# 168 products that nothing reads, put behind the last gated product of an encoder trunk

## The chip, the cores and the metric

The kernel runs on one core of one Trainium2 chip (trn2). The metric is the device time of one execution in microseconds (us); less is better. A core has five engines that work through a queue of instructions each: TensorE (PE; its weight loads are shown apart as PEld), VectorE (DVE), ScalarE (ACT), GpSimd (POOL) and SyncE (SP), which issues most DMAs here.

## The reference, cut to what matters

Two layers of attention, gates and a feed-forward network over 256 tokens of width 2048, all in float32. The change stands at the very end, behind the last gated embedding product and beside the last norm:

```python
for i in range(DEPTH):
    ...
    e = p[i] @ w_ple_in[i]
    x = x + jax.nn.sigmoid(rmsnorm(x, g_ple[i]) @ w_ple_gate[i]) * e
return rmsnorm(x, g_final)
```

`rmsnorm(x, g)` is `x * rsqrt(mean(x*x) + eps) * g`. The output is 1 x 256 x 2048.

## The kernel before

Activations are kept transposed: `xT` holds x as 16 chunks of 128 partitions (features) by 256 tokens. A product of 128 output features therefore runs over 16 chunks of the contraction, and its result, 128 x 256, gathers in one PSUM bank.

To get float32 accuracy out of a faster matmul type, every operand is held as two parts, a rounded high part and the rest. For activations the two stand side by side in one tile of 512 columns: `ua[j]` and `ub[j]` (16 tiles each), high part in columns 0 to 255, low part in 256 to 511. For weights `piece` (L159) loads 128 x 1024 floats into `w`, ScalarE makes `whi`, and VectorE makes `wlo`. `emit` (L191) then issues, for each chunk, the kernel's own form: one matmul with `whi` as the stationary operand over all 512 columns (L199), which gives high x high in the first half of the bank and high x low in the second; and one with `wlo` over the 256 high columns (L200), which adds low x high to the second half. A branch of it (L195 to L197, `whole`) does the same with three matmuls of 256 columns into one half. The two halves are added later by `joined` (ScalarE copies one half, VectorE adds the other).

Products go through four PSUM banks in turn (`ps_mm`). The value products (L385 to L387) have activations as the stationary operand and 512 columns of weights as the moving one. Attention scores (L334) take both operands from activation tiles (`fa`, `fb`, `ub`, `kr`).

The stage around the change is the last loop of the second layer: 16 gated products (L676 to L687), each with a sigmoid on ScalarE, a multiply with `es` and an add to `xT` on VectorE, and then `add(n)` (L670), which squares the chunk into one of two sums and scales the chunk by `g_final`. The last of the 16 uses the `whole` form. After the loop, `norm` (L259) sums the squares over partitions with four fp32 matmuls of one column (L264), VectorE works out the reciprocal root, `spread` (L267) brings it to all partitions with one fp32 matmul of 128 x 256 (L273), and six multiplies over `xT` (L72, called from L690 to L693) are each followed by an output DMA from SyncE.

The order of each engine's queue is set by the Tile framework's scheduler, which orders instructions by a timeline of its own; dependencies between engines become semaphore waits. `tt` (L71) is the helper behind most VectorE operations, so many of these carry the line L72.

Of the kernel before, what the change touches and what calls it, by code (L numbers as in the profile page):

```python
# [13 lines left out]
F32R = mybir.dt.float32r  # L14
I32 = mybir.dt.int32
AF = mybir.ActivationFunctionType
# [3 lines left out]
P = 128  # L20
T = 256
# [15 lines left out]
PT = 8  # L37
# [13 lines left out]
def encoder(ctx, tc, x, p, positions, cols, lams, wq, wk, wv, wcq, wckv, wkr, wga, wgb,  # L51
            w_q_up, w_kn, w_v, w_bd, w_bm, w_out, w_gate, w_up, w_down, w_pin, w_pg, rope_c, out):
    nc = tc.nc
    V, A, PE = nc.vector, nc.scalar, nc.tensor
# [3 lines left out]
    wts = pool("wts")  # L58
    tmp = pool("tmp")
    stat = pool("stat")  # L60
    ps_mm = pool("ps_mm", 4, space=PSUM)
# [6 lines left out]
    def bank(ps=ps_at, tag="at", name="at", shape=(P, 2 * T)):  # L68
        return ps.tile(list(shape), F32, tag=tag, name=name)

    def tt(o, a, b, op):  # L71
        return V.tensor_tensor(out=o, in0=a, in1=b, op=op)  # L72
# [4 lines left out]
    def ts(o, a, s1, s2, op0, op1=ALU.bypass):  # L77
        return V.tensor_scalar(out=o, in0=a, scalar1=s1, scalar2=s2, op0=op0, op1=op1)


    ua = [const.tile([P, 2 * T], F32R, name=f"ua{j}") for j in range(NC)]
    ub = [const.tile([P, 2 * T], F32R, name=f"ub{j}") for j in range(NC)]
# [11 lines left out]
    xT = const.tile([P, NC, T], F32, name="xT")  # L94
# [4 lines left out]
    at = 0  # L99
# [19 lines left out]
    def tables():  # L119
        V.tensor_copy(posf, posi)  # L120
        got = []
        for i, name in enumerate("pm"):
            ang, k, r, a = (aside[j + i][:, m, :] for j in (1, 3) for m in range(2))
            ts(ang, posf, rc[:, 2 * i : 2 * i + 1], None, ALU.mult)
            ts(k, ang, 1.0 / TWO_PI, ROUND, ALU.mult, ALU.add)
            ts(k, k, ROUND, None, ALU.subtract)
            stt(r, k, -C1, ang, ALU.mult, ALU.add)
            stt(r, k, -C2, r, ALU.mult, ALU.add)
            stt(r, k, -C3, r, ALU.mult, ALU.add)
            ts(r, r, PI_IN, -PI_IN, ALU.min, ALU.max)  # L130
            stt(a, r, -1.0, r, ALU.mult, ALU.min)
            ts(a, a, math.pi / 2, None, ALU.add)
            cs = const.tile([P, T], F32, name="cos_" + name)
            sn = const.tile([P, T], F32, name="sin_" + name)
            A.activation(cs, a, AF.Sin)
            A.activation(sn, r, AF.Sin)
            ts(sn, sn, rc[:, 2 * i + 1 : 2 * i + 2], None, ALU.mult)
            got += [cs, sn]
        return got
# [62 lines left out]
    def product(src, us, whole=False):  # L202


        acc = bank(ps_mm, "mm", "mm")
        n = len(us)
        for a in range(0, n, PT):
            m = min(PT, n - a)
            hi, lo = piece(src[:, a * P : (a + m) * P], m)
            emit(acc, hi, lo, 0, us[a : a + m], a == 0, a + m == n, whole)  # L210
        return acc[:, :T] if whole else acc
# [15 lines left out]
    def joined(acc, o=None):  # L227
        t = scratch("join", 3)
        A.activation(t, acc[:, T:], AF.Copy)  # L229
        o = scratch("a", 4) if o is None else o  # L230
        tt(o, acc[:, :T], t, ALU.add)
        return o
# [7 lines left out]
    def rsqrt(src, n, eps, width):  # L240

        v, y, a = (stat.tile([P, 2 * DH], F32, tag="r" + s, name="r" + s, bufs=2)[:, :width] for s in "vya")
        ts(v, src, 1.0 / n, eps, ALU.mult, ALU.add)
        ts(y.bitcast(I32), v.bitcast(I32), -0.5, 1597463007.0, ALU.mult, ALU.add)
        for _ in range(3):
            stt(a, y, -0.5, y, ALU.mult, ALU.mult)
            tt(a, a, v, ALU.mult)
            stt(y, a, 1.5, y, ALU.add, ALU.mult)
        return y

    def square_into(acc, src, first):
        if first:
            A.activation(acc, src, AF.Square)
        else:
            sq = scratch("sq", 2)
            A.activation(sq, src, AF.Square)
            tt(acc, acc, sq, ALU.add)

    def norm(sums, n):  # L259

        s = bank()
        for j, a in enumerate(sums):
            for b in range(2):
                PE.matmul(s[:, b : b + 1], a[:, b * P : (b + 1) * P], ones[:, 0:1], start=j + b == 0, stop=j + b == len(sums))  # L264
        return rsqrt(s[:, 0:2], n, EPS, 2)

    def spread(col, copied=True):  # L267

        dg = stat.tile([P, 2, P], F32, tag="dg", name="dg", bufs=1)
        for b in range(2):  # L270
            ts(dg[:, b, :], ident, col[:, b : b + 1], None, ALU.mult)
        s = bank()
        PE.matmul(s[:, :T], ones, dg, start=True, stop=True)  # L273
        if not copied:
            return s[:, :T]
        row = stat.tile([P, T], F32, tag="row", name="row", bufs=2)
        A.activation(row, s[:, :T], AF.Copy)  # L277
        return row

    def normed(sums, one, two):  # L280

        got = [joined(one())]
        col = norm(sums, DM)
        got.append(joined(two()))
        return spread(col), col, got
# [4 lines left out]
    def stream(us, gain):  # L290

        acc = squares()

        def add(c):
            split(us[c], xT[:, c, :], g(gain, c))
            square_into(acc, xT[:, c, :], c == 0)

        return acc, add
# [70 lines left out]
    def values(src, us, load=None):  # L369
# [3 lines left out]
        for half in range(2):  # L373
# [18 lines left out]
            if not half:  # L392
                yield vals


    warm = bank()
    for _ in range(WARM):
# [7 lines left out]
    for L in range(DEPTH):  # L405

        steps = values(wv[L], ua, None if L else load)
        for vd in steps:
            if L == 0 and vd is not None:
# [3 lines left out]
                with after_splits():  # L413
                    rcol = norm([sq0[0][:, j, :] for j in range(2)], DM)
                    next(steps)
                    R = spread(rcol)
                    cos_p, sin_p, cos_m, sin_m = tables()
                    lambdas()
                break
            if L:  # L420
                next(steps)
                rcol = norm([acc], DM)
                next(steps)
                R = spread(rcol)
                break
# [5 lines left out]
        for o, t in ((cr, cos_p), (sr, sin_p), (crm, cos_m), (srm, sin_m)):  # L431
            tt(o, t, R, ALU.mult)

# [17 lines left out]
        def latent(us, w, raws):  # L451
            ss = squares()
            for c in range(len(us)):
                tt(raws[c], joined(product(w[L, c], ua)), R, ALU.mult)
                square_into(ss, raws[c], c == 0)
# [55 lines left out]
        def gate(w, store, n):  # L511
            tt(store(n), joined(product(w[L, n], ua)), R, ALU.mult)

# [115 lines left out]
        acc, add = stream(ub, f"g_ffn{L}")  # L629
# [4 lines left out]

        R, _, pre = normed([acc], lambda: product(w_gate[L, 0], ub), lambda: product(w_up[L, 0], ub))
        pT, es = ua[14:], []
# [4 lines left out]
        for part, (f0, f1) in enumerate(FF_PARTS):  # L641
# [11 lines left out]
            if last:  # L653
                acc, add = stream(ub, f"g_ple{L}")
# [10 lines left out]
        R, _, pre = normed([acc], lambda: product(w_pg[L, 0], ub), lambda: product(w_pg[L, 1], ub))  # L665
# [8 lines left out]
        else:  # L674
            acc, add = stream(ua, f"g_mix{L + 1}")
# [11 lines left out]
            add(n)  # L687

    R = spread(norm(sums, DM), copied=False)
    for n, m in ((0, 1), (1, 1), (2, 2), (4, 4), (8, 4), (12, 4)):  # L690
        o = xT[:, n : n + m, :]
        tt(o, o, R[:, None, :].to_broadcast([P, m, T]), ALU.mult)
        nc.sync.dma_start(out[:, n : n + m, :], o)  # L693
# [84 lines left out]
```

## Time and profile before

| | us |
|---|---|
| median of 2 runs | 2939.7 (2939.02 to 2940.39) |
| the profiled execution's own time | 2939.35 |
| its span, first to last instruction | 2937.4 |
| TensorE busy | 2918.8 |
| VectorE busy | 2039.8 |
| ScalarE busy | 1520.5 |

The profile is of one execution. A page of it gives the busy time of each engine, the chain of work that ended last, and groups of equal instructions. A group's line reads: line of the code, engine, operation, output <- inputs, shape, count | busy time, mean of one in ns | idle time before. Matmuls are pipelined and their ends are modelled, so the durations of neighbours overlap; the pace is read from starts, or from counts in a window. Rows of the timeline begin with the start and the duration in us; what stands in brackets is the idle time of the engine before the row and what ended it. Rows of the chain have a start, a length and what the chain went through. Rows of the windows have the stretch, its length, busy time and count for PE, PEld, DVE, ACT and POOL, then the granted TensorE clock, the DMA share and GB/s.

### The profile page before, as it was taken

What the parts mean: (1) busy time and instruction counts of PE and PEld (TensorE: products, weight loads), DVE (VectorE), ACT (ScalarE), POOL (GpSimd) and SP (SyncE); (2) the same over time, 40 slices, a digit from 0 to 9 for tenths busy, and PEclk for the clock granted to TensorE, in tenths of its full rate; (3) what the DMA queues carried; (4) which work ended last, traced back from release to release, by engine and by line L of the source; (5) the groups of instructions that cost most, each with busy time, mean ns of one, the idle gap of its engine ahead of it and who ended that gap; (6) DMA issues with size and microseconds to landing.
All of it is one profiled execution on the core that took longest, in us unless ns stands there. A gap on an engine that the chain in (4) does not pass through costs nothing.

```text
span 2937.4 us, 45159 instructions
## 1 busy us (share of the span) xinstructions
PE 2918.8 (99%) x17390; PEld 2583.1 (88%) x17390; DVE 2039.8 (69%) x3447; ACT 1520.5 (52%) x2512; POOL 3.5 (0%) x11
## 2 busy tenths in 40 slices
PE   9999999999999999999999999999999999999998
PEld 7998888888888888888889988888888888888887
DVE  7887658776666656666858875587666666566676
ACT  6576545554444444444646755455444444444454
POOL 0000000000000000000000000000000000000000
PEclk9999999999999999999999999999999999999999
DMA  6544455555565566566554444555556655655654
GB/s 229 166 159 144 158 188 192 188 185 187 182 194 187 177 191 195 188 188 187 187 186 160 152 151 165 187 192 188 185 188 183 193 187 180 193 187 188 188 186 141
DMA packets 155751, 532.47 MB, mean 181 GB/s; under 512 B 16928, under 2 KB 23584, under 8 KB 155536
## 3 DMA queue, kind: packets, MB, share of 16 engines
q1 hardware_dynamic: 154944, 528.55, 56.1%
q8 instruction: 136, 2.23, 0.3%
q0 software_dynamic: 160, 0.46, 0.1%
q10 hardware_dynamic: 432, 0.59, 0.1%
q14 instruction: 79, 0.65, 0.1%
HBM read 527.43 MB, written 2.10 MB: 180 GB/s over the span
## 4 chain that ended last, share of the span: by engine, by line
PE 99%; DVE 0%; DMA 0%; ACT 0%; SPq 0%; issue 0%; DVEq 0%
PE mm L199 56%; PE mm L200 29%; PE mm L195 3%; PE mm L197 3%; PE mm L196 3%; PE S L334 1%; PE mmv L385 1%; PE mmv L386 1%; PE mmv L387 1%; PE at L352 0%; PE at L552 0%; PE at L609 0%; DMA w<-in_wv 0%; PE at L273 0%; DVE xT L72 0%; PE at L312 0%
## 5 line engine op out<-in xcount | busy, mean ns | idle before, releaser
L72 DVE TENSOR_TENSOR wlo<-w,whi 128x1024 fp32r<-128x1024 f32 (+2 forms) x1029 | 1229.4, 1195 | 785.3 <-ACT whi L169 772.6
L169 ACT ACTIVATE whi<-w 128x1024 fp32r<-128x1024 f32 (+2 forms) x1029 | 1066.0, 1036 | 1332.1 <-issue 778.8
L199 PE MATMUL mm<-ub,whi 128*128 128x512 f32 x3920 | 1379.0, 394 | 0.0
L200 PE MATMUL mm<-ub,wlo 128*128 128x256 f32 x3920 | 1109.3, 283 | 0.0
L199 PE MATMUL mm<-ua,whi 128*128 128x512 f32 x3136 | 1104.3, 394 | 0.0
L200 PE MATMUL mm<-ua,wlo 128*128 128x256 f32 x3136 | 885.9, 283 | 0.0
L199 PEld LDWEIGHTS mm<-ub,whi 128*128 128x128 f32 x3920 | 736.1, 188 | 169.5
L200 PEld LDWEIGHTS mm<-ub,wlo 128*128 128x128 f32 x3920 | 737.0, 188 | 0.2
L199 PEld LDWEIGHTS mm<-ua,whi 128*128 128x128 f32 x3136 | 588.4, 188 | 132.4
L200 PEld LDWEIGHTS mm<-ua,wlo 128*128 128x128 f32 x3136 | 589.6, 188 | 1.4
L195 PE MATMUL mm<-ua,whi 128*128 128x256 f32 x608 | 173.0, 285 | 0.0
L197 PE MATMUL mm<-ua,wlo 128*128 128x256 f32 x608 | 172.4, 284 | 0.0
L196 PE MATMUL mm<-ua,whi 128*128 128x256 f32 x608 | 171.3, 282 | 0.0
L72 DVE TENSOR_TENSOR a<-mm,join 128x256 f32<-128x256 f32 x371 | 155.1, 418 | 0.4 <-ACT join L229 0.2
L72 DVE TENSOR_TENSOR xT<-xT,mm 128x256 f32<-128x256 f32 x256 | 106.8, 420 | 51.7 <-PE mm L200 47.9
L229 ACT ACTIVATE join<-mm 128x256 f32<-128x256 f32 x371 | 136.3, 367 | 5.3 <-PE mm L200 5.3
L195 PEld LDWEIGHTS mm<-ua,whi 128*128 128x128 f32 x608 | 114.6, 188 | 1.3
L197 PEld LDWEIGHTS mm<-ua,wlo 128*128 128x128 f32 x608 | 114.5, 188 | 0.5
L196 PEld LDWEIGHTS mm<-ua,whi 128*128 128x128 f32 x608 | 114.5, 188 | 0.0
L72 DVE TENSOR_TENSOR a<-a,row 128x256 f32<-128x256 f32 x207 | 87.4, 425 | 6.6 <-ACT row L277 0.8
L385 PE MATMUL mmv<-whi,ua 128*128 128x512 f32 x128 | 51.7, 404 | 4.2 <-ACT whi L169 4.2
L72 DVE TENSOR_TENSOR a<-a 128x256 f32<-128x256 f32 x120 | 51.0, 425 | 4.0
(162 smaller groups left out, 1497.8 us busy)
## 6 DMA issues: line engine op xcount, KB each, us to landing
w<-in_w_gate SPq DMA_DIRECT2D x176, 512.0 KB, 4.4
w<-in_w_up SPq DMA_DIRECT2D x176, 512.0 KB, 4.5
w<-in_w_down SPq DMA_DIRECT2D x128, 512.0 KB, 3.8
w<-in_wga SPq DMA_DIRECT2D x64, 512.0 KB, 3.7
w<-in_wgb SPq DMA_DIRECT2D x64, 512.0 KB, 3.9
w<-in_w_out SPq DMA_DIRECT2D x64, 512.0 KB, 4.5
w<-in_w_pg SPq DMA_DIRECT2D x64, 512.0 KB, 4.0
w<-in_w_down SPq DMA_DIRECT2D x64, 384.0 KB, 3.5
```

Of the source, the lines that this page charges most:

```text
L72: return V.tensor_tensor(out=o, in0=a, in1=b, op=op)
L169: last_split[:] = A.activation(hi[:, :m], w[:, :m], AF.Copy), tt(lo[:, :m], w[:, :m], hi[:, :m].bitcast(F32), ALU.subtract)
L195: PE.matmul(acc[:, :T], hi[:, s], u[:, :T], start=start, stop=False)
L196: PE.matmul(acc[:, :T], hi[:, s], u[:, T:], start=False, stop=False)
L197: PE.matmul(acc[:, :T], lo[:, s], u[:, :T], start=False, stop=stop)
L199: PE.matmul(acc, hi[:, s], u, start=start, stop=False)
L200: PE.matmul(acc[:, T:], lo[:, s], u[:, :T], start=False, stop=stop)
L229: A.activation(t, acc[:, T:], AF.Copy)
L334: PE.matmul(S[:, b, :], q[:, b * P : (b + 1) * P], k, start=j == 0, stop=j == len(pairs) - 1)
L385: PE.matmul(banks[b], xh, hi[:, s], start=a + j == 0, stop=False)
L386: PE.matmul(banks[b], xl, hi[:, s], start=False, stop=False)
L387: last_mm[:] = [PE.matmul(banks[b], xh, lo[:, s], start=False, stop=a + j == n - 1)]
```

## The change

A function `others` is added and called once, behind the norm and spread of the last loop and ahead of the six output multiplies. It issues 168 products in the kernel's types: eleven blocks of 12 in the own form (a 512-column matmul and a 256-column one for each), and three blocks of 12 with the 512-column matmul alone. Three single fp32 matmuls stand behind the latter. Nothing reads any of the results. Stationary operands are 128 columns of `ub[j]`, moving ones `ua[j]` or a new tile `side`, a rounded copy of four chunks of `xT`. The blocks differ in the element at which the stationary operand starts ("later"), in that of the moving one ("moved"), in the half of the bank that the second matmul adds to ("first"), in the tile of the second stationary operand ("apart"), and in the order of the matmuls over two banks ("pairs", "turns").

```diff
+    def others():
+        N = 12
+        side = wts.tile([P, PT * P], F32R, tag="whi", name="side", bufs=3)
+        A.activation(side, xT[:, :4, :].rearrange("p c t -> p (c t)"), AF.Copy)
+
+        def blocks(name, hi, lo, x, low=T):
+            acc = bank(ps_mm, "mm", name)
+            for j in range(N):
+                PE.matmul(acc, hi(j), x(j), start=j == 0, stop=False)
+                PE.matmul(acc[:, low : low + T], lo(j), x(j)[:, :T], start=False, stop=j == N - 1)
+
+        at = lambda n: lambda j: ub[j][:, n : n + P]
+        own = lambda j: ua[j]
+        blocks("usual", at(0), at(P), own)
+        blocks("later16", at(16), at(P + 16), own)
+        blocks("later8", at(8), at(P + 8), own)
+        blocks("later32", at(32), at(P + 32), own)
+        blocks("moved0", at(0), at(P), lambda j: side[:, 0:512])
+        blocks("moved16", at(0), at(P), lambda j: side[:, 16:528])
+        blocks("moved8", at(0), at(P), lambda j: side[:, 8:520])
+        blocks("first", at(0), at(P), own, 0)
+        blocks("apart", at(0), lambda j: ub[15 - j][:, P : 2 * P], own)
+        two = [bank(ps_mm, "mm", "pairs") for _ in range(2)]
+        for j in range(0, N, 2):
+            for i in range(2):
+                PE.matmul(two[i], at(0)(j + i), ua[j], start=j == 0, stop=False)
+            for i in range(2):
+                PE.matmul(two[i][:, T:], at(P)(j + i), ua[j][:, :T], start=False, stop=j == N - 2)
+        two = [bank(ps_mm, "mm", "turns") for _ in range(2)]
+        for j in range(0, N, 2):
+            for i in range(2):
+                PE.matmul(two[i], at(0)(j + i), ua[j], start=j == 0, stop=False)
+                PE.matmul(two[i][:, T:], at(P)(j + i), ua[j][:, :T], start=False, stop=j == N - 2)
+        for _ in range(3):
+            acc = bank(ps_mm, "mm", "wide")
+            for j in range(N):
+                PE.matmul(acc, ub[j][:, :P], ua[j], start=j == 0, stop=j == N - 1)
+            acc = bank(ps_mm, "mm", "gap")
+            PE.matmul(acc[:, :T], xT[:, 0, :P], xT[:, 1, :], start=True, stop=True)
...
     R = spread(norm(sums, DM), copied=False)
+    others()
     for n, m in ((0, 1), (1, 1), (2, 2), (4, 4), (8, 4), (12, 4)):
         o = xT[:, n : n + m, :]
         tt(o, o, R[:, None, :].to_broadcast([P, m, T]), ALU.mult)
```

## The prediction

> **What bounds the kernel now.** I read the page first: busy shares, then the chain that ended last.
>
> ```profile
> span 2937.4 us, 45159 instructions
> PE 2918.8 (99%) x17390; PEld 2583.1 (88%) x17390; DVE 2039.8 (69%) x3447; ACT 1520.5 (52%) x2512; POOL 3.5 (0%) x11
> ...
> PE 99%; DVE 0%; DMA 0%; ACT 0%; SPq 0%; issue 0%; DVEq 0%
> ```
>
> TensorE is the chain: whatever is put into its queue lengthens the kernel by its own time, except where TensorE sits idle. So two things are needed: the pace of the added forms, and the idle time at the place where they go in.
>
> For the pace of the kernel's own form (a 512-column product with `whi`, then a 256-column one with `wlo`) I take the groups by line over 200 us that hold nothing else on TensorE (window 700 to 900).
>
> ```profile
> L199 PE MATMUL mm<-ub,whi 128*128 128x512 f32 x346 | 121.6, 393 | 0.0
> L200 PE MATMUL mm<-ub,wlo 128*128 128x256 f32 x347 | 98.1, 283 | 0.0
> L199 PE MATMUL mm<-ua,whi 128*128 128x512 f32 x224 | 78.5, 393 | 0.0
> L200 PE MATMUL mm<-ua,wlo 128*128 128x256 f32 x224 | 63.0, 283 | 0.0
> ```
>
> The means (393 and 283 ns) overlap and are no pace. The counts are: 570 pairs in 200 us, 0.351 us a pair, with `ua` or `ub` as the moving operand.
>
> For the place, the timeline of the end, TensorE's rows and those of VectorE (DVE) that matter:
>
> ```profile
> 2915.61 0.39 PE L199 MATMUL mm<-ub,whi 128*128 128x512 f32 x1
> 2915.83 0.28 PE L200 MATMUL mm<-ub,wlo 128*128 128x256 f32 x1
> ...
> 2921.53 0.28 PE L197 MATMUL mm<-ub,wlo 128*128 128x256 f32 x1
> ...
> 2921.65 0.50 PE L264 MATMUL at<-ones,ssq 128*128 128x1 f32 x4
> 2921.85 0.42 DVE L72 TENSOR_TENSOR a<-mm,row 128x256 f32<-128x256 f32 x1 [2.12 <-PE mm L197]
> ...
> 2924.14 0.61 PE L264 MATMUL at<-ones,ssq 128*128 128x1 f32 x4 [1.99 <-ACT ssq L253]
> 2924.79 0.16 DVE L78 TENSOR_SCALAR rv<-at 128x2 f32<-128x2 f32 x1 [1.15 <-PE at L264]
> ...
> 2927.49 1.22 PE L273 MATMUL at<-dg,ones 128*128 128x256 f32 x2 [2.73 <-DVE dg L78]
> 2928.74 4.75 DVE L72 TENSOR_TENSOR xT<-xT,at 128x256 f32<-128x256 f32 x6 [1.32 <-PE at L273]
> ```
>
> The last gated product's matmuls stop issuing at 2921.65. Then TensorE mostly waits for a small chain (gate, sum of squares, norm, spread) until the six output multiplies start at 2928.74. That is 7.09 us in which added matmuls cost nothing; all after it is paid for.
>
> **The change, part by part.** It adds 132 products in the own form (eleven blocks of 12: one 512-column matmul and one of 256), 36 products of 512 columns alone ("wide"), three fp32 matmuls of 128x256 ("gap"), and one ScalarE copy ("side"). It removes nothing. In the order of the built program all the rest of every engine's queue stands as before, but for two neighbouring VectorE steps of chunk 14 that change places. Nothing goes to a DMA queue.
>
> *Where they end up on TensorE.* In the built order all come behind the last gated matmul. The norm's matmuls (L264, L273) stand among them: the first two behind 8 pairs and half of the next, the other two behind 15 pairs, the spread's behind 19 more. They come late rather than early: the second two are reached 15 x 0.351 + 0.45 = 5.7 us after 2921.65, while their input was ready at 2924.14, 2.5 us after; the spread is reached 19 x 0.351 = 6.7 us behind these, while before it was 2927.49 - 2924.14 = 3.35 us. So TensorE never waits. VectorE runs its norm under the products.
>
> *What waits for them.* The gap matmuls read chunks 0 and 1 of `xT`, which the first two output multiplies overwrite. In the build the first multiply waits for TensorE's last increment, which is that of the third gap. Behind it in VectorE's queue stand the five other multiplies, and behind these SyncE's six output DMAs. So the whole end (2928.74 to 2937.4) moves behind the last gap.
>
> *The 132 pairs.* 132 x 0.351 = 46.33 us. Their weights lie in `ub` and their moving operand in `ua` or `side`, where the kernel has `whi`/`wlo` and `ub`/`ua`. Nearest rows for other tiles, from the chain of waits and from the timeline of the same stretch:
>
> ```profile
> 1697.73 1.43 PE S L334 x12
> ...
> 1697.92 0.52 PE L334 MATMUL S<-kr,ub 128*128 128x256 f32 x3
> 1698.28 0.52 PE L334 MATMUL S<-fb,fa 128*128 128x256 f32 x3
> ```
>
> 1.43 / 12 = 0.119 us for 256 columns, with operands in `fa`, `fb`, `kr` and `ub`. In the own form the step from an L200 to the next product is also 0.12 (2921.53 to 2921.65 for L197). Four other places give the same pace, so I take 0.351 for the blocks at other tiles. No row has an operand that starts 8, 16 or 32 elements into a tile. For both ends: the steps of the own form in the timeline vary between 0.22 and 0.24 for 512 columns (2915.61 to 2915.83 is 0.22) and I allow 0.11 to 0.13 for 256, so a pair between 0.33 and 0.37, and 132 of them within 2.6 us either way. "Pairs" and "turns" only reorder 512- and 256-column matmuls, and "first" writes the low product to the first half of the bank, as L195 to L197 do.
>
> *The 36 wide ones.* The nearest rows are the value products, all of 512 columns and each with a weight load of its own:
>
> ```profile
> 1483.61 0.39 PE L385 MATMUL mmv<-whi,ua 128*128 128x512 f32 x1
> ...
> 1486.40 0.40 PE L385 MATMUL mmv<-whi,ua 128*128 128x512 f32 x1
> ```
>
> The rows between them make 12 steps: 2.79 / 12 = 0.2325 us. 36 x 0.2325 = 8.37 us; by the steps 0.22 to 0.24 it lies between 7.9 and 8.6.
>
> The Trainium skill, TensorE: Matmul & The Clock Gate, section "Back-to-back issue gap", gives a warm gap of N / 2.4 + 2.5 ns, 215.7 for 512 columns and 109.2 for 256. An estimate from it is 0.325 a pair and 50.7 us for pairs and wide together instead of 54.7; this trace's 0.351 and 0.2325 are longer, and the measurement decides.
>
> *The fp32 ones in the stream.* From the chain of waits, earlier in the kernel, where they stand between other products:
>
> ```profile
> 1392.09 0.43 PE at L273 x2
> ...
> 1479.84 0.34 PE at L264 x4
> 1480.18 0.34 PE mmv L385
> 1480.52 0.23 PE mmv L386
> ...
> 1692.82 0.43 PE at L312 x2
> ```
>
> A 128x256 fp32 matmul takes 0.43 (L273, L312). Two of L264 take 0.34, and the product behind them 0.34 for 0.23: 0.45 together. So 0.43 each for the first two gaps, 0.43 for the moved spread, 2 x 0.45 for the four norm matmuls that now stand in the stream: 2.19 us.
>
> *The last gap.* From its first row to the output multiply:
>
> ```profile
> 1391.93 0.59 PE L273 MATMUL at<-dg,ones 128*128 128x256 f32 x2
> ...
> 2921.65:2928.74 7.09, 2.33 (x12) 1.44 (x10) 3.53 (x16) 1.34 (x3) 0.00 (x0) 0.79 0.00 0
> 2928.74:2937.40 8.66, 0.00 (x0) 0.00 (x0) 4.75 (x6) 0.00 (x0) 0.00 (x0) 0.50 0.62 242
> ```
>
> 0.59 us in a busy stream (it took 1.22 at the end of before, where the window's granted clock is 0.79 on the mean and then 0.50), plus the hand-over of about 0.03 seen between 2927.49 + 1.22 and 2928.74. I take 0.62.
>
> *The side copy* is a 128x1024 pass on ScalarE:
>
> ```profile
> 2913.23 1.06 ACT L169 ACTIVATE whi<-w 128x1024 fp32r<-128x1024 f32 x1 [0.63 <-PE mm L199]
> ...
> 2916.15 0.38 ACT L229 ACTIVATE join<-mm 128x256 f32<-128x256 f32 x1 [1.56 <-PE mm L200]
> ```
>
> It takes a `whi` buffer whose last reader is the L199 of 2915.61, so it runs from about 2915.85 to 2916.9, and the join of chunk 14 waits behind it 0.75 us. The cover is VectorE's 2.12 us of idling ahead of 2921.85: the steps of chunk 14 still end before it. Without that cover it would cost 0.75. I take nothing.
>
> **The sum.** 46.33 + 8.37 + 2.19 = 56.89 us from 2921.65 to the start of the last gap, 2978.54; plus 0.62, the multiplies start at 2979.16 instead of 2928.74: 50.4 us later, and all behind them keeps its 8.66 us. The profiled execution took 2939.35 us for its span of 2937.4; that becomes 2989.8, 1.7% more. The median of the runs shown is 2939.7 (2939.02 to 2940.39), so the base adds less than 1 us of doubt. With the bounds above (2.6 for the pairs, 0.3 to 0.5 for wide, 0.75 for side) the forecast's own range is 2986.5 to 2993.5.
>
> **The rivals.**
> 1. *The own form's pace comes from its places or its order.* If some of the places or orders tried lose less between products, they run quicker: with all eleven blocks at the lowest steps, 0.33 and 0.22, the time is 2989.8 - 2.8 - 0.4 = 2986.6. Against it: L334 and L195 to L197 have other tiles and other orders at the same 0.12. Chance 0.13, for 2986 to 2988. By the section of the Trainium skill named above, the gap on TensorE: Matmul & The Clock Gate, every added product would run so, and its estimate ends at 2985.8; no row of this trace has that pace.
> 2. *A shifted operand exposes its weight load.* The five blocks "later16", "later8", "later32", "moved16", "moved8" have 120 matmuls whose operand starts off the places known from the trace. What an uncovered load costs is bounded by 128x128 products, which have one load each and little else to stream:
>
> ```profile
> 1696.84 0.89 PE at L552 x8
> ```
>
> 0.89 / 8 = 0.111 us. With that on all 120: 13.3 us, 2989.8 + 13.3 = 3003.1, over 2% slower. The point from which it decides is 8.7 us, 0.07 a matmul. Against it: TensorE's operands at other starts (halves and quarters of a tile) keep the pace. Chance 0.10, of which 0.06 over 2%; shifts of which a part costs end between 2991 and 2998.
> 3. *Nothing is added, or it is hidden.* Not slower only if the products do not run, since what is idle at the end is 7.09 us against 57: unread results could be left out, 2939.4. The built order holds all 303 matmuls and the multiply's wait. If the multiplies did not wait for the gaps, the program would end with TensorE, at about 2979.2 + 1.9 = 2981.1. Together 0.03.
>
> **How the numbers follow.** Forecast 0.74, rivals 0.13, 0.10 and 0.03. The likeliest time is 2989.8. The range 2985.5 to 2994.5 is the forecast's own, 2986.5 to 2993.5, with 1 us for the base on either side; it holds rival 1 and a small part of rival 2. A measurement of this kernel is taken to tell a change from none at about 2%, here 58.8 us over 2939.7, or 2998.5: the forecast lies 8.7 us under it. Over 2% slower is the large part of rival 2, and a sum that misses something of that size: 0.10. Faster by over 2% has no mechanism: 0.01. Within 2%: 0.89.
>
> **What would show it.** In the timeline of the changed kernel: no idle row on TensorE from the last gated matmul to the third gap; blocks of 12 pairs 4.2 us long whatever their name; wide blocks 2.8 us; the first output multiply released by the gap matmul near 2979; 8.7 us behind it. Blocks that differ by name by more than 0.02 us a pair would speak for rivals 1 or 2; a wait of L264 or L273 on VectorE, or multiplies that start before the last gap, would make the reckoning of the place wrong.

## The result, and the profile after

The changed kernel takes 2989.6 us (median of 2 runs, 2989.5 to 2989.7) against 2939.7: a ratio of 1.0168, 95% interval 1.0151 to 1.0185. That is 49.9 us more; 2989.8 was forecast.

The page of the changed kernel, the lines that answer to those of before:

```profile
span 2987.8 us, 45773 instructions
...
PE 2975.2 (100%) x17696; PEld 2632.4 (88%) x17696; DVE 2039.0 (68%) x3447; ACT 1521.4 (51%) x2513; POOL 3.5 (0%) x11
...
PE 99%; DMA 0%; DVE 0%; SPq 0%; ACT 0%; DVEq 0%; issue 0%
```

TensorE has 306 matmul records more (an fp32 matmul has two) and is still the whole chain. The end of its timeline, with ScalarE's and VectorE's rows that matter:

```profile
2916.12 1.06 ACT L400 ACTIVATE side<-xT 128x1024 fp32r<-128x1024 f32 x1 [1.44 <-PE mm L199]
2917.09 0.36 ACT L229 ACTIVATE join<-mm 128x256 f32<-128x256 f32 x1
...
2921.63 0.28 PE L197 MATMUL mm<-ub,wlo 128*128 128x256 f32 x1
2921.75 0.40 PE L405 MATMUL usual<-ua,ub 128*128 128x512 f32 x1
2921.94 0.42 DVE L72 TENSOR_TENSOR a<-mm,row 128x256 f32<-128x256 f32 x1 [1.09 <-PE mm L197]
...
2924.75 0.50 PE L264 MATMUL at<-ones,ssq 128*128 128x1 f32 x4
2927.42 0.50 PE L264 MATMUL at<-ones,ssq 128*128 128x1 f32 x4
2934.57 0.59 PE L273 MATMUL at<-dg,ones 128*128 128x256 f32 x2
...
2952.49 0.39 PE L405 MATMUL first<-ua,ub 128*128 128x512 f32 x1
2956.73 0.40 PE L405 MATMUL apart<-ua,ub 128*128 128x512 f32 x1
2960.97 0.40 PE L422 MATMUL pairs<-ua,ub 128*128 128x512 f32 x1
2965.15 0.40 PE L428 MATMUL turns<-ua,ub 128*128 128x512 f32 x1
2969.31 0.40 PE L433 MATMUL wide<-ua,ub 128*128 128x512 f32 x1
...
2978.44 0.59 PE L435 MATMUL gap<-xT 128*128 128x256 f32 x2
2979.07 4.74 DVE L72 TENSOR_TENSOR xT<-xT,at 128x256 f32<-128x256 f32 x6 [48.46 <-PE gap L435]
```

No TensorE row has idle time in brackets: the norm's matmuls (L264, L273) never wait. VectorE has the norm done long before and then idles 48.46 us for the third gap. The windows give the same: from the first added product to the multiplies TensorE is busy for 57.28 of 57.32 us at a granted clock of 1.00. The span of 2987.8 ends 8.73 us behind the multiplies' start, where before it was 8.66.

```profile
2921.75:2979.07 57.32, 57.28 (x318) 49.34 (x316) 3.54 (x17) 1.35 (x3) 0.00 (x0) 1.00 0.00 1
```

The blocks are not all alike, though. From the starts above, "first" and "apart" take 4.24 us for 12 pairs, 0.3533 a pair; "pairs" 4.18, 0.3483; "turns" 4.16, 0.3467. The total was right while single blocks lie 0.7% above 0.351 and 1.2% below it. That is what most of the experiments are about.

### The profile page after: what moved, and what is told of

It reads as the page before. It is cut to its first block, busy times and chain, and to the rows that moved or that the text cites. A ratio compares the mean times of both kernels' runs of the same rounds, so it can differ in the third digit from the quotient of the medians.

```text
span 2987.8 us, 45773 instructions
## 1 busy us (share of the span) xinstructions
PE 2975.2 (100%) x17696; PEld 2632.4 (88%) x17696; DVE 2039.0 (68%) x3447; ACT 1521.4 (51%) x2513; POOL 3.5 (0%) x11
## 4 chain that ended last, share of the span: by engine, by line
PE 99%; DMA 0%; DVE 0%; SPq 0%; ACT 0%; DVEq 0%; issue 0%
PE mm L199 55%; PE mm L200 28%; PE mm L195 3%; PE mm L197 3%; PE mm L196 3%; PE S L334 1%; PE mmv L385 1%; PE mmv L386 1%; PE mmv L387 1%; PE at L352 0%; PE at L594 0%; PE at L651 0%; PE later L405 0%; PE moved L405 0%; PE wide L433 0%; DMA w<-in_wv 0%
## 5 line engine op out<-in xcount | busy, mean ns | idle before, releaser
L199 PE MATMUL mm<-ub,whi 128*128 128x512 f32 x3920 | 1379.0, 394 | 0.0
L200 PE MATMUL mm<-ub,wlo 128*128 128x256 f32 x3920 | 1109.3, 283 | 0.0
L199 PE MATMUL mm<-ua,whi 128*128 128x512 f32 x3136 | 1104.3, 394 | 0.0
L200 PE MATMUL mm<-ua,wlo 128*128 128x256 f32 x3136 | 886.0, 283 | 0.0
L199 PEld LDWEIGHTS mm<-ub,whi 128*128 128x128 f32 x3920 | 736.2, 188 | 169.4
L200 PEld LDWEIGHTS mm<-ub,wlo 128*128 128x128 f32 x3920 | 737.2, 188 | 0.2
L199 PEld LDWEIGHTS mm<-ua,whi 128*128 128x128 f32 x3136 | 588.4, 188 | 132.4
L200 PEld LDWEIGHTS mm<-ua,wlo 128*128 128x128 f32 x3136 | 589.7, 188 | 1.4
L197 PE MATMUL mm<-ua,wlo 128*128 128x256 f32 x608 | 172.4, 284 | 0.0
L197 PEld LDWEIGHTS mm<-ua,wlo 128*128 128x128 f32 x608 | 114.5, 188 | 0.5
```

The costliest lines, as they stand in the source:

```text
L197: PE.matmul(acc[:, :T], lo[:, s], u[:, :T], start=False, stop=stop)
L199: PE.matmul(acc, hi[:, s], u, start=start, stop=False)
L200: PE.matmul(acc[:, T:], lo[:, s], u[:, :T], start=False, stop=stop)
```

## The experiments

### The end waits for the last gap

```diff
-            PE.matmul(acc[:, :T], xT[:, 0, :P], xT[:, 1, :], start=True, stop=True)
+            PE.matmul(acc[:, :T], ones, cos_m, start=True, stop=True)
```

> The changed kernel, but the three gap matmuls read constant tiles instead of chunks 0 and 1 of xT, so the output multiplies wait for the spread alone. Theory (the end waits for the last gap): the multiplies start when the spread is through, near 2935.2, and run under the products; the program ends with TensorE near 2979.1, and with the 1.95 us between span and time it takes about 2981, some 8.5 us less than the changed kernel. Rival (the multiplies' wait is not what holds the end, all that counts is the length of TensorE's queue plus the output): the time stays at 2989.6.

2980.8 us, ratio to before 1.0141 (1.0127 to 1.0155): 8.8 us less than the changed kernel. In its timeline the multiplies are released by the spread:

```profile
2933.90 0.60 PE L273 MATMUL at<-dg,ones 128*128 128x256 f32 x2
...
2934.53 4.74 DVE L72 TENSOR_TENSOR xT<-xT,at 128x256 f32<-128x256 f32 x6 [4.60 <-PE at L273]
```

The theory holds and the rival is out. The last 8.8 us of the change's price are not TensorE's time at all, but the output's, put behind three matmuls that read `xT`.

### One block alone

```diff
+    def others():
+        acc = bank(ps_mm, "mm", "usual")
+        for j in range(12):
+            PE.matmul(acc, ub[j][:, :P], ua[j], start=j == 0, stop=False)
+            PE.matmul(acc[:, T:], ub[j][:, P : 2 * P], ua[j][:, :T], start=False, stop=j == 11)
...
     R = spread(norm(sums, DM), copied=False)
+    others()
```

> The kernel before with one block of 12 pairs alone (4.2 us of TensorE), no side copy and no gap matmuls. In the built order the second pair of the norm's matmuls stands behind the whole block. Theory A (the 7.09 us at the end are free): the time is that of before, 2939.7. Theory B (only idle time ahead of the next matmul in the queue's order is free): the second pair of the norm starts 12 x 0.351 + 0.45 = 4.7 us after the last gated matmul instead of 2.5, so 2.2 us more, near 2941.9; up to 0.6 us less if the spread runs at the full clock.

2940.7 us against 2939.3, ratio 1.0004 (0.9995 to 1.0013): the medians are 1.4 us apart, between the two theories, and the interval holds both. The time does not tell them apart. The timeline can:

```profile
2921.01 0.28 PE L197 MATMUL mm<-ub,wlo 128*128 128x256 f32 x1
...
2925.74 0.50 PE L264 MATMUL at<-ones,ssq 128*128 128x1 f32 x4
...
2930.24 4.74 DVE L72 TENSOR_TENSOR xT<-xT,at 128x256 f32<-128x256 f32 x6 [1.31 <-PE at L273]
```

From the last gated matmul (L197) to the multiplies it takes 9.23 us, where before it took 2928.74 - 2921.53 = 7.21. So 4.2 us of products cost 2.0, although in the kernel before TensorE waits there for 1.99 + 2.73 = 4.72 of the 7.09 us: the second pair of the norm stands behind the block, and the wait of 2.73 for the spread's input comes after it as before. Theory B, by this one profile; idle time is free only ahead of the matmul that ends it.

### Long blocks: is the pace the form's?

```diff
...
+        usual("lead")
+        for k, form in enumerate(forms):
+            usual("usual" + "ABCD"[k])
+            form("A")
+        usual("usualE")
+        for k, form in enumerate(forms):
+            gap("gap" + "ABCD"[k])
+            usual("split" + "ABCD"[k])
+            gap("pag" + "ABCD"[k])
+            form("B")
...
```

The four entries of `forms` are first, apart, later by 16 and kern, in this order.

> Long blocks of 36 pairs in place of the change's: a usual block ahead of and behind each of the forms first, apart, later by 16 elements, and kern (weights in the whi and wlo buffers, moving operand ub, as the kernel itself has it); then the same forms again, each behind a gap matmul and followed or led by a usual block behind a gap. Two ScalarE copies fill the weight buffers. Theory (the pace belongs to the form's places): every usual block runs at 0.346 us a pair wherever it stands, first, apart and later at 0.353, kern at 0.351, the same in both halves. Rival (the pace is a phase that the queue has fallen into and keeps): a usual block behind first runs at 0.353, and a gap matmul in front changes the pace of the same form by 0.003 or more. In either case the whole takes 18 x 36 x 0.350 = 227 us more than before and some 3 us for eight gaps, less the 7 us of idle time: near 3163.

3156.7 us, 6 less than expected. First matmuls of some blocks in its timeline:

```profile
2949.01 0.39 PE L405 MATMUL firstA<-ua,ub 128*128 128x512 f32 x1
...
2986.45 0.39 PE L405 MATMUL usualC<-ua,ub 128*128 128x512 f32 x1
2998.94 0.39 PE L405 MATMUL laterA<-ua,ub 128*128 128x512 f32 x1
3011.65 0.40 PE L405 MATMUL usualD<-ua,ub 128*128 128x512 f32 x1
3024.37 0.39 PE L405 MATMUL kernA<-ub,side 128*128 128x512 f32 x1
3037.01 0.39 PE L405 MATMUL usualE<-ua,ub 128*128 128x512 f32 x1
3049.73 0.59 PE L410 MATMUL gapA<-cos_m,ones 128*128 128x256 f32 x2
...
3101.66 0.58 PE L405 MATMUL splitC<-ua,ub 128*128 128x512 f32 x1
3114.33 0.59 PE L410 MATMUL pagC<-cos_m,ones 128*128 128x256 f32 x2
...
3127.71 0.58 PE L405 MATMUL splitD<-ua,ub 128*128 128x512 f32 x1
3140.62 0.59 PE L410 MATMUL pagD<-cos_m,ones 128*128 128x256 f32 x2
```

First, usual B and apart, the three blocks from 2949.01 to 2986.45, take 37.44 us, 0.3467 a pair, and usual C 12.49, 0.3469; later takes 0.3531, kern 0.3511. But usual D and usual E, the same instructions as C, take 12.72 us each, 0.3533. Behind a gap the usual block of 3101.66 takes 12.67 us, some 0.19 of them the gap's, so its pace is the quick one; so it is for the usual block behind usual E's gap. That of 3127.71, which comes after a later block and a gap, takes 12.91, 0.007 a pair more. So a gap does not always bring the quick pace back.

Neither theory holds alone. The usual form has two paces at the same places, and both theory and rival have a part: the slower one was seen in this run only behind blocks of later and kern, but what decides between the two is not shown. "First" and "apart", at 0.3533 in the changed kernel, run at 0.3467 here; the simplest reading is that they had the second pace there.

### The starts, scanned

In the built program the addresses of `ua` and `ub` leave a remainder of 128 when divided by 256 bytes, and those of `whi`, `wlo` and `side` leave none. So the changed kernel's forms can be ordered by how far the weights start behind the moving operand, counted in 256 bytes (the offset): usual 0, later8 32, later16 and moved16 64, moved8 96, later32, moved0 and the kernel's own 128. The three moved blocks have the same weights and only another start of the moving operand; they begin at 2939.90, 2944.10 and 2948.33 and take 0.350 (moved0), 0.3525 (moved16) and 0.3467 (moved8) a pair. So the start of the weights alone does not set the pace.

```diff
...
+        steps = (0, 8, 16, 24, 32, 40, 48, 56, 64, 96, 128)
+        block("lead", 0)
+        for n in steps:
+            block(f"up{4 * n}bytes", n)
+        for n in reversed(steps):
+            block(f"down{4 * n}bytes", n)
...
```

The steps are counted in floats of 4 bytes.

> Blocks of 36 pairs at eleven starts of the stationary operand (0 to 256 bytes in steps of 32, 384 and 512 bytes), each behind a gap matmul, once with the starts rising and once falling. Theory (pace by offset, period 256 bytes): 0.3467 at 0, 256 and 512, 0.3535 at 32, 0.3533 at 64, 0.3512 at 128 and 384, and the same rising and falling. Rival (pace kept from the block before): rising and falling differ at the same start by 0.004 or more. Time near 2939 + 23 x 12.6 + 23 x 0.43 - 7 = 3232 either way.

3223.7 us, 8 less than expected. First matmuls of most blocks of the rising half in its timeline; from one start to the next lie 36 pairs and a gap of 0.43:

```profile
2934.55 0.58 PE L405 MATMUL up0bytes<-ua,ub 128*128 128x512 f32 x1
2947.47 0.58 PE L405 MATMUL up32bytes<-ua,ub 128*128 128x512 f32 x1
2960.61 0.59 PE L405 MATMUL up64bytes<-ua,ub 128*128 128x512 f32 x1
2973.74 0.58 PE L405 MATMUL up96bytes<-ua,ub 128*128 128x512 f32 x1
2986.67 0.58 PE L405 MATMUL up128bytes<-ua,ub 128*128 128x512 f32 x1
2999.72 0.59 PE L405 MATMUL up160bytes<-ua,ub 128*128 128x512 f32 x1
3012.75 0.58 PE L405 MATMUL up192bytes<-ua,ub 128*128 128x512 f32 x1
3025.91 0.58 PE L405 MATMUL up224bytes<-ua,ub 128*128 128x512 f32 x1
3038.82 0.58 PE L405 MATMUL up256bytes<-ua,ub 128*128 128x512 f32 x1
3051.74 0.58 PE L405 MATMUL up384bytes<-ua,ub 128*128 128x512 f32 x1
```

(12.92 - 0.43) / 36 = 0.347 at 0, and likewise 0.353 at 32 and 64, 0.347 at 96, 0.351 at 128, 0.350 at 160, 0.354 at 192, 0.347 at 224 and 256. The falling half gives the same at every start to within 0.001, and 0.351 at 384 and 0.347 at 512 in both. The theory holds with its period of 256 bytes; behind a gap, in this order, nothing was kept from the block before. Offset 0 came out quick in every such block here, where the long blocks had shown both of its paces.

### The kernel before, with its weights moved

```diff
     wts = pool("wts")
+    wts.tile([P, 32], F32, tag="shift", name="shift", bufs=1)
```

> The kernel before with an empty tile of 128 bytes a partition ahead of the weight buffers, and nothing else. Theory (the pace of the own form goes by where the weights start against the moving operand, counted in 256 bytes: 0.3467 us a pair at 0, 0.3512 at 128, 0.3533 at 64): whi and wlo now start at the same offset as ua and ub, where before they were 128 bytes apart, so the 7056 pairs run at 0.3467 and the time falls by 7056 x 0.0045 = 32 us to 2907.5. Rival A (the pace is a phase that the queue keeps and the kernel's many waits set it): no change, 2939. Rival B (with waits and transposes in between, the pairs fall into the other pace seen at offset 0, 0.3533): 15 us more, 2954.

> The same with an empty tile of 192 bytes: the weights start 64 bytes behind the moving operand in 256. Theory (pace by offset): 0.3533 us a pair as in the blocks later by 16 elements, 7056 x 0.0021 = 15 us more, 2954. Rival A: no change, 2939.

128 bytes: 2934.1 us, ratio 0.9981 (0.9972 to 0.999). 192 bytes (48 floats): 2949.7, ratio 1.0038 (1.0025 to 1.0051). The second goes the way of the theory, with 10.6 us more instead of 15. The first gained 5 us, not 32. Its groups by line in two windows of 200 us, the 512-column matmuls alone (L200 here, L199 before, since a line was added above):

```profile
L200 PE MATMUL mm<-ub,whi 128*128 128x512 f32 x354 | 122.8, 394 | 0.0
L200 PE MATMUL mm<-ua,whi 128*128 128x512 f32 x224 | 77.6, 394 | 0.0
...
L200 PE MATMUL mm<-ub,whi 128*128 128x512 f32 x417 | 147.4, 399 | 0.0
L200 PE MATMUL mm<-ua,whi 128*128 128x512 f32 x130 | 46.2, 399 | 0.0
```

From 700 to 900 there are 578 pairs, 0.346 each. From 1050 to 1250 there are 547, with 20 products of the `whole` form that take some 7.1 us (20 x 0.357): (200 - 7.1) / 547 = 0.353. The kernel before has 550 pairs and 20 such products in that window, 0.351 a pair. At offset 0 the kernel has both paces, one in each of these windows: rival B's pace in part of the stages. So I tried the two other offsets at which blocks had shown only the quick one, 224 and 96.

> The kernel before with an empty tile of 96 bytes ahead of the weight buffers: weights start 224 bytes behind the moving operand, counted in 256. Theory (each offset has the paces that its blocks showed; at 224 only 0.3467 was seen, both rising and falling): 7056 x 0.0045 = 32 us less, 2907.5, with 0.3467 in every stage of products. Rival (as at offset 0, the queue falls into 0.3533 in some stages whatever the offset): between 2907 and 2954, near 2934 if half of the stages do.

> The same with 224 bytes: weights start 96 bytes behind. Theory: at 96 only 0.3467 was seen, 2907.5. Rival: between 2907 and 2954.

96 bytes: 2905.8 us (2905.57 to 2907.41), ratio to before 0.9888 (0.9872 to 0.9905). 224 bytes: 2908.1, ratio 0.9894 (0.9879 to 0.9909). The first in the window from 1050 to 1250, where the tile of 128 bytes had the slow pace:

```profile
L200 PE MATMUL mm<-ub,whi 128*128 128x512 f32 x453 | 157.1, 390 | 0.0
L200 PE MATMUL mm<-ua,whi 128*128 128x512 f32 x109 | 38.0, 390 | 0.0
```

562 pairs and 16 products of the `whole` form, (200 - 16 x 0.357) / 562 = 0.346: the quick pace. An empty tile of 96 bytes makes a kernel that is quicker than the one before and the changed one. The tile also moves `w` and the scratch tiles that lie behind the weights. That the weights make the difference rests on the scan, where nothing else moved, and on the size: 32 us were expected, and 33.1 and 30.9 came.

### What a matmul costs beside its columns

```diff
...
+        for n in (512, 448, 384, 320, 256, 192, 128):
+            single(f"c{n}x", n)
+        single("half512x", 512, 64)
+        single("half256x", 256, 64)
+        single("same512x", 512, P, True)
+        single("same256x", 256, P, True)
...
```

> Blocks of 36 single matmuls at 512 to 128 moving columns, with 64 instead of 128 stationary columns, with the same stationary operand each time, and the pair and the single matmuls in bfloat16, each behind a gap matmul. Theory (a matmul costs a fixed part on top of its columns, tied to the change of weights): the step falls in a straight line from 0.228 at 512 to 0.118 at 256, with 0.01 or more over at every width, no lower than the 0.111 of a weight load; with 64 stationary columns the part over the columns shrinks by half. Rival (each column costs more than at the full clock, as a share): the part over falls in proportion to the columns, and 64 stationary columns change nothing. In bfloat16 both expect a shorter part over the columns; by the Trainium skill, TensorE: Matmul & The Clock Gate, section Back-to-back issue gap, an estimate of 0.216 and 0.109, or 0.325 a pair.

3027.2 us. First matmuls of some of its blocks in the timeline, each behind a gap:

```profile
2953.79 0.49 PE L409 MATMUL c320x<-ua,ub 128*128 128x320 f32 x1
2959.50 0.47 PE L409 MATMUL c256x<-ua,ub 128*128 128x256 f32 x1
2964.24 0.44 PE L409 MATMUL c192x<-ua,ub 128*128 128x192 f32 x1
2968.69 0.41 PE L409 MATMUL c128x<-ua,ub 128*128 128x128 f32 x1
2973.14 0.58 PE L409 MATMUL half512x<-ua,ub 128*64 128x512 f32 x1
2981.86 0.47 PE L409 MATMUL half256x<-ua,ub 128*64 128x256 f32 x1
...
2999.97 0.38 PE L421 MATMUL bfpair<-low 128*128 128x512 bf16 x1
3012.11 0.38 PE L427 MATMUL bf512x<-low 128*128 128x512 bf16 x1
3020.31 0.38 PE L427 MATMUL bf256x<-low 128*128 128x256 bf16 x2
```

With the gap taken off and over 36, a step is 0.147 us at 320 columns, 0.120 at 256, and 0.112 at 192 and at 128. From 320 to 256 that is 0.00042 a column, which leaves 0.012 at no columns: a fixed part, and a floor near 0.112. Up to 512 the steps stay within 0.003 of that line (0.173 at 384, 0.203 at 448, 0.228 at 512). So far the theory. Its second half holds only in part. With 64 stationary columns the step is 0.114 at 256, where the part over the columns does shrink by about half, but (8.72 - 0.43) / 36 = 0.230 at 512, no less than the 0.228 with 128. The blocks with the same stationary operand each time take 0.228 and 0.120, no less than with changing ones; as the trace still has a weight load of 188 ns for each of their matmuls, they do not test the change of weights. What the part at 512 columns is made of stays open.

In bfloat16 the step is 0.216 at 512 and the pair takes 0.325, as estimated from the Trainium skill (TensorE: Matmul & The Clock Gate, section "Back-to-back issue gap"). The fixed part in the Trainium skill's formula is 0.0025 us, and bfloat16 fits it. The kernel's float32 type has about 0.012.

## Why the prediction was right

*The place.* The forecast had 56.89 us from the first added matmul to the last gap and 0.62 to the multiplies, 57.51; it took 57.32. The norm's matmuls came late and not early, as worked out. One sentence was wrong: that added matmuls cost nothing in the 7.09 us. TensorE waits for only 4.72 of them, in two pieces, and one block alone cost 2.0 us for 4.2. In the changed kernel the sum went by TensorE's continuous stream, so this did not enter.

*The wait.* The first multiply is released by the third gap, and the run with gaps that read other tiles took 8.8 us off.

*The pairs.* 46.33 us were forecast. From 2921.75 to 2969.31 are 47.56 us, less 0.90 and 0.43 for the norm's matmuls: 46.23. The sum was right and the reason behind it was not: "four other places give the same pace" held for score matmuls of 256 columns, and was carried to every block. Rival 1's mechanism, a pace that comes from the places, is real; it is worth from -0.0045 to +0.002 us a pair around the kernel's 0.351 instead of the -0.02 that the rival was priced at. The eleven blocks fell on both sides, and their mean came to 46.23 / 132 = 0.350. That they nearly cancel is luck, but luck of little worth: all 132 pairs at the quick pace would have been 132 x 0.0045 = 0.6 us less, well inside the range.

*The wide ones.* 8.37 forecast; 2969.31 to 2978.44 less two gaps of 0.43 is 8.27.

*The fp32 ones* took what their rows in the stream said, 0.43 and 0.45; the last gap took 0.63 to the multiplies, where 0.62 was taken.

*Side.* It ran at 2916.12, some 0.3 us later than the 2915.85 worked out, and moved the join to 2917.09. VectorE's idle time ahead of the last gate fell from 2.12 to 1.09 and was not used up.

*Rival 2*, a weight load in the open, priced at 0.111 a matmul, did not happen: the worst start costs 0.002 a pair more than the kernel's own in the changed kernel, and 0.003 in the scan.

## What to carry to other kernels

Price added work on the bounding engine by its pace in the stream (counts in a window), not by the mean duration of its rows, and look separately for what waits for its last instruction: here three matmuls that nobody reads held back the output. Idle time on a queue is free only ahead of the instruction that ends it, as the one block showed. Where thousands of equal matmuls are the chain, try the start of the weight buffers against the moving operand's, over all starts in 256 bytes and in the whole kernel: 1.1% lay in an empty tile of 96 bytes.

## What the runs showed of the hardware

The pace of the own form goes by the weights' start behind the moving operand's, counted in 256 bytes: 0.347 us a pair at 0, 96 and 224, 0.350 to 0.351 at 128 and 160, 0.353 to 0.354 at 32, 64 and 192. At 0 there are two paces, 0.347 and 0.353, and the kernel with the tile of 128 bytes had each through a window of 200 us. What in the chip makes the offset count, and what decides between the two paces, no run here shows; in the long blocks the second was seen behind blocks at other offsets (64 and 128), once even across a gap matmul. The Trainium skill (TensorE: Matmul & The Clock Gate, section "Step-by-step: what each phase is for") says that loading the next weights takes no read bandwidth from the running matmul. These runs show a step that depends on how the two operands lie to each other, by up to 2%; whether read bandwidth is the reason they do not show.
